# Moving one product of a two-tile feature pair, and starting its inner form one pair later

## The chip, the core and the metric

The kernel runs on one core of a Trainium2 chip. The metric is the device time of one execution in microseconds (us), the median of several runs. The engines are called TensorE (PE in the profile; PEld is its weight load), VectorE (DVE), ScalarE (ACT), GpSimd (POOL) and SyncE (SP, which here only issues DMAs).

## The reference, cut to what matters

One step of a hybrid decoder layer: a feed-forward network (FFN), a mixer (HGRN2 and Mamba-2 heads), a second FFN, a final norm. There are 1048 token rows (16 meta, 1024 prompt and 8 sample rows); the second FFN works on 1032 of them, since the meta rows are dropped. The change lies in the two FFNs alone:

```python
def swiglu(x, wg, wu, wd):
    return (jax.nn.silu(x @ wg) * (x @ wu)) @ wd
...
    h = h + 0.5 * swiglu(rmsnorm(h, n1), w1g, w1u, w1d)
...
    h = h + 0.5 * swiglu(rmsnorm(h, n2), w2g, w2u, w2d)
```

The model width is 1024 (8 blocks of 128), the FFN's width 2816 (22 feature tiles of 128). Everything is float32.

## The kernel before

**Arithmetic.** Each float32 factor is split into a high part (`hi`, a cast on ScalarE) and the remainder (`lo`, a subtraction on VectorE), and each product is made by three matmuls, hi x hi, hi x lo and lo x hi (`mm3`, L163 to L165).

**The seven products.** For one feature tile gate and up are computed together as a 2 x 2 by 2 x 2 block product in Winograd's form: seven products instead of eight, numbered 1 to 7, each over 4 blocks of 128 rows. The token columns are cut in two halves c = 0, 1, and each half in two quarters of Q columns (Q = 262 in the first FFN, 258 in the second). One *step* is one product for one half: 4 blocks x 3 matmuls = 12 matmuls of Q columns. The order of a tile is `ORDER = (1, 6, 2, 5, 7, 3, 4)`, two steps each. Products 1 and 2 are added up in one PSUM tile, 5 and 3 in one, 7 and 4 in one; 6 has its own. Such a tile ("acc") is a pair of banks, one for each half, and the pool has two of these pairs.

After the second half of a product, `post` in `pair` reads the PSUM pair: product 1 is copied by ScalarE (L675); 6 makes `v` (VectorE, L677); 2 is scaled to `g0` (L670) and goes through SiLU on ScalarE (L682); 5 makes `x` (L684); 7 makes `u1` (L686, then a scaling, L670); 3 makes `g1`; 4 makes `u0` (L699 in the inner form, L704 otherwise, then L670), and then the products gate x up are written (`product_`, L719).

**Pairs and the inner form.** The 22 tiles are taken as 11 pairs, numbered from 0. Pairs 0 and 1 are plain: two tiles with seven products each, 2 x 14 steps. From pair 2 on (the fifth tile) a pair is in the *inner form*: product 3 is left out of both tiles (`ORDER6`), and the two tiles' products 3 are made together, again in Winograd's form, as seven inner products of 6 matmuls each, in the "mis" banks (`Inner`, two at a step, the last one alone). An inner pair has thus 24 steps of 12 matmuls and 42 inner matmuls, 330 instead of 336. The first tile is products 1, 6, 2, 5, 7, 4; the second 1, 6, 2, 5, 7, then inner (1, 6) and (5, 7), then 4, then inner (2, 3) and (4). The SiLU of the third part and the last product of both tiles ("gates", `inner.then`) run in the first steps of the next pair.

`Inner.operands` builds once in each FFN, on VectorE (11 operations) and ScalarE (3 casts), the sums of the split token blocks that the inner products need, in the steps of pair 1, and one more operand (a cast and a remainder) in pair 2.

**The order of the work.** Inside an FFN the order on every engine is written out by hand. `Steps` is a list of TensorE's steps; `S.before(i, fn)` puts work ahead of step i, and what a step's `post` issues comes behind it. The engines run their queues in order and wait for one another by semaphores, so the list fixes only the order on each queue. `Left.plan` places a tile's weights: four loads (SyncE, L452) 11 and 10 steps ahead of the tile, the Winograd sums 5, 6, 7, 3 (VectorE, L458) 7 to 5 steps ahead, each cast (L462) 4 steps and each remainder (L466) 3 steps ahead of its product. `Hidden.jobs` makes the differences of the pair's results for the down projection (L816) and stores them to DRAM (SyncE, L819). Weights lie in 8 raw buffers ("r") and 6 split ones ("ws").

The program in these functions:

Of the kernel before, what the change touches and what calls it, by code (L numbers as in the profile page):

```python
# [313 lines left out]
ORDER = (1, 6, 2, 5, 7, 3, 4)  # L314
# [126 lines left out]
class Left:  # L441
# [27 lines left out]
        self.hi(p)  # L469
        self.lo(p)  # L470

    def plan(self, S, s0, late, sums, order=ORDER, last=0):
        n = len(order)
        his = [2 * i - 4 + late + last * (i == n - 1) for i in range(n)]
        for ps, ds, fn in (
            ((1, 7, 4, 2), (-11, -11, -10, -10), self.load),
            ((5, 6, 7, 3), [d + sums for d in (-7, -7, -6, -5)], self.sum_),
            (order, his, self.hi),
            (order, [d + 1 for d in his], self.lo),
        ):  # L480
            for p, d in zip(ps, ds):
                S.before(s0 + d, lambda p=p, fn=fn: fn(p))
# [9 lines left out]
class Unit:  # L492
# [25 lines left out]
    def both(self, S):  # L518
        for p in ORDER:
            for c in range(2):  # L520
                self.step(S, p, c, (0, 1))
# [6 lines left out]
ORDER6 = (1, 6, 2, 5, 7, 4)  # L528
# [121 lines left out]
def pair(K, S, wg, wu, f, ops, spread, hid, late_r, first=None, inner=None):  # L650

    nc = K.nc
    fs = slice(f * P, f * P + P)
    s0 = len(S.steps)
    wait = late_r > 14
    tm = {}  # L660
    left = Left(K, [wg[:, 0:4, fs], wu[:, 0:4, fs], wu[:, 4:8, fs], wg[:, 4:8, fs]], 4)

    def temp(n, cs):
        if n not in tm:
            tm[n] = halves(K.t(2 * K.Q))
        return tm[n][:, cs]

    def times_r(n, i, cs, src=None):
        t = temp(n, cs)
        nc.vector.tensor_mul(t, t if src is None else src, spread.lanes(i, cs))  # L670
        return t

    def post(p, cs, b):
        if p == 1:
            nc.scalar.copy(temp("z", cs), b)  # L675
        elif p == 6:
            nc.vector.tensor_add(temp("v", cs), b, temp("z", cs))  # L677
        elif p == 2 and (f == 0 or wait and f == 1):
            nc.scalar.copy(temp("g0", cs), b)
        elif p == 2:  # L680
            t = times_r("g0", 0, cs, b)
            nc.scalar.activation(t, t, AF.Silu)  # L682
        elif p == 5:
            nc.vector.tensor_add(temp("x", cs), b, temp("v", cs))  # L684
        elif p == 7:
            nc.vector.tensor_add(temp("u1", cs), b, temp("x", cs))  # L686
            if inner:
                times_r("u1", 1, cs)
        elif p == 3:
            nc.vector.tensor_add(temp("g1", cs), b, temp("v", cs))  # L690
            if f == 0:
                return
            if wait and f == 1:
                silu(0, cs)
            silu(1, cs)
            times_r("u1", 1, cs)
        elif inner:
            t = temp("v", cs)
            nc.vector.tensor_add(t, b, t)  # L699
            tm["u0"] = tm["v"]  # L700
            times_r("u0", 0, cs)
            product_(0, cs)
        else:
            nc.vector.tensor_add(temp("u0", cs), b, temp("v", cs))  # L704
            if f == 0:
                return
            times_r("u0", 0, cs)
            for n in range(2):
                product_(n, cs)

    def silu(n, cs):
        t = times_r(f"g{n}", n, cs)
        nc.scalar.activation(t, t, AF.Silu)  # L713

    def product_(n, cs):
        if "h" not in tm:
            tm["h"] = True
            hid.append(K.slot("s", K.T))
        nc.vector.tensor_mul(halves(hid[0][:, n * 2 * K.Q : n * 2 * K.Q + 2 * K.Q])[:, cs], temp(f"g{n}", cs), temp(f"u{n}", cs))  # L719

    if inner:
        i = f % 2
        left.plan(S, s0, 0, 0, ORDER6, 2 * i)
        unit = Unit(K, left.w, [o.op for o in ops], 4, post)

        def both(*ps):
            for p in ps:
                for c in range(2):
                    unit.step(S, p, c, (0, 1))

        def keep():
            inner.raw[i] = left.raw[3]

        cs = slice(0, 2)

        def gate():
            tm["g1"] = tm["x"]
            silu(1, cs)

        S.before(s0 - 4, keep)  # L740
        inner.then[i] = (gate, lambda: product_(1, cs))
        inner.out[i] = lambda: temp("x", cs)
        if i == 0:
            both(*ORDER6)
            return
        S.before(s0 + 1, lambda: inner.begin(S, s0))
        both(1, 6, 2, 5, 7)
        inner.step(S, 1, 6)
        inner.step(S, 5, 7)
        both(4)  # L750
        inner.step(S, 2, 3)
        inner.step(S, 4)
        e = len(S.steps)
        for at, fn in enumerate((inner.then[0][0], inner.then[1][0], inner.then[0][1], inner.then[1][1])):
            S.before(e + at, fn)
        return

    if not first:
        left.plan(S, s0, int(f == 1), 3 * int(f == 1))
        Unit(K, left.w, [o.op for o in ops], 4, post).both(S)  # L760
        return

    late = {}

    def post_first(p, cs, b):

        if p == 5:
            late[p] = b
        else:
            post(p, cs, b)  # L770
            if p == 6:
                post(5, cs, late[5])

    order = first(S, left)
    unit = Unit(K, left.w, [o.op for o in ops], 4, post_first)
    for ps_ in (order[:6], order[6:]):
        for c in range(2):
            for p in ps_:
                unit.step(S, p, c, (c,), True)
    cs = slice(0, 2)  # L780
    for i, (fn, *args) in enumerate(((silu, 0, cs), (silu, 1, cs), (times_r, "u0", 0, cs), (product_, 0, cs), (times_r, "u1", 1, cs), (product_, 1, cs))):
        S.before(s0 + late_r + i, lambda fn=fn, args=args: fn(*args))


FP = DFF // P // 2
# [5 lines left out]
class Hidden:  # L791
# [6 lines left out]
    def jobs(self, S, i, hid, e0, e1, inner):  # L798

        K = self.K  # L800
        t, b = {}, {}

        def block(n):

            return hid[n // 2][0][:, n % 2 * 2 * self.K.Q : n % 2 * 2 * self.K.Q + 2 * self.K.Q]

        def val(p):
            return b[p] if p in b else block({1: 0, 12: 1, 2: 2, 3: 3}[p])

        def sub(p, x, y):  # L810
            s = {5: 0, 6: 0, 7: 1, 4: 1}[p]
            if s not in t:
                t[s] = K.slot("s", self.K.T)
            o = (p in (6, 4)) * 2 * self.K.Q
            b[p] = t[s][:, o : o + 2 * self.K.Q]
            K.nc.vector.tensor_sub(b[p], val(x), val(y))  # L816

        def store(p):
            K.nc.sync.dma_start(self.d[p][:, :, i, :], halves(val(p)))  # L819

        ats = (e0 + 1, e1 + 1, e1 + 3, e1 + 5) if not inner else (e1 + 4, e1 + 5, e1 + 7, e1 + 9) if i < FP - 1 else (e1 + 4, e1 + 5, e1 + 6, e1 + 7)
        for at, args in zip(ats, ((5, 12, 1), (6, 3, 5), (7, 3, 12), (4, 2, 6))):
            S.before(at, lambda args=args: sub(*args))
            S.before(at + 2, lambda p=args[0]: store(p))
        for at, p in ((e0 + 2, 1), (e1 + (5 if inner else 1), 3), (e1 + 2, 2)):
            S.before(at, lambda p=p: store(p))

    def load(self, S, p, at):
# [147 lines left out]
def ffn(K, wg, wu, wd, ops, spread, src, first, after, late_r):  # L976
# [9 lines left out]
    with K.tc.manual_schedule(engines={E.PE, E.DVE, E.Activation, E.SP}):  # L986
        S = Steps()
        S.before(14, lambda: K.banks(2))
        hidden = Hidden(K)
        inner = Inner(K, ops)  # L990
        for i in range(NF // 2):
            hid, e = [], []
            rec = inner.next() if i >= 2 else None
            if i == 1:
                def operands(s0=len(S.steps)):
                    made, late = inner.operands()
                    for n, fn in enumerate(made):
                        S.before(s0 + 5 + 2 * n + n // 4, fn)
                    for n, fn in enumerate(late):
                        S.before(s0 + 36 + 2 * n, fn)  # L1000

                S.before(len(S.steps) + 4, operands)
            for f in (2 * i, 2 * i + 1):
                hid.append([])
                pair(K, S, wgv, wuv, f, ops, spread, hid[-1], late_r, first if f == 0 else None, rec)
                e.append(len(S.steps))
            hidden.jobs(S, i, hid, *([late_r + 6, max(late_r + 7, e[1])] if i == 0 else e), rec)
        h = []
        down(K, S, wdv, hidden, src, h, after)
        S.run()  # L1010
# [1253 lines left out]
```

## Time and profile before

| | |
|---|---|
| median of 3 runs | 2013.61 us (2012.29 to 2014.58) |
| the profiled execution | 2017.68 us, span 2016.0 us |
| granted TensorE clock, mean | 0.986 |
| TensorE busy | 1939.5 us (96%) |
| VectorE busy | 1543.0 us (77%) |
| ScalarE busy | 860.3 us (43%) |
| first FFN: pairs 1 and 2 | 78.45 to 124.05 us and 124.05 to 169.63 us |
| second FFN: pairs 1 and 2 | 1354.07 to 1394.37 us and 1394.37 to 1439.17 us |

Times in the profile count from the start of the span. A row of the timeline or of a group names engine, line, operation, tiles and shapes; a bracket at its end is the time that the engine stood idle just before, and what ended it. In a row by window stand the window, its length, the busy time and number of instructions of each engine, TensorE's granted clock, the share of the DMA engines and GB/s. In the list of waits stand who waited for whom, the sum in us, how often, and the longest. Matmuls overlap, and their ends are modelled, so the idle time shown is somewhat shorter than the time from one matmul's start to the next would say.

### The profile page before, as it was taken

The numbers are of one execution on the slowest core, as the hardware profiler recorded it, in microseconds if no ns is written. First come the engines' busy times: TensorE is split into PE (matmuls) and PEld (weight loads), VectorE is DVE, ScalarE is ACT, GpSimd is POOL, SyncE is SP. The second block draws the span as 40 slices with busy tenths as digits, with TensorE's granted clock in tenths as the row PEclk, the third lists the DMA queues.
The fourth block names the chain that finished last, engine by engine and source line by source line (L and its number), as shares of the span: only waits on it lengthen the run. The fifth ranks groups of instructions, "written<-read, shape, count | busy, mean of one in ns | idle before, by whom it ended". The sixth has DMA issues, their size and how long they took to land.

```text
span 2016.0 us, 40978 instructions
## 1 busy us (share of the span) xinstructions
PE 1939.5 (96%) x16573; PEld 1898.7 (94%) x16573; DVE 1543.0 (77%) x2744; ACT 860.3 (43%) x1653; POOL 85.0 (4%) x135
## 2 busy tenths in 40 slices
PE   7999999999999999999999999999999999999997
PEld 7989999999999999998988989999999999999997
DVE  7778888888788877576655447888888888878973
ACT  7523232223543644465543535743232322354352
POOL 4000000000000410000000001200000000000000
PEclk8999999999999999999998999999999999999999
DMA  7223233335877542232622154223232333487851
GB/s 215 77 88 102 85 105 100 95 96 157 252 248 245 158 151 55 58 100 71 169 77 75 56 165 135 73 91 112 79 106 85 105 101 103 143 236 245 272 180 65
DMA packets 323877, 258.45 MB, mean 128 GB/s; under 512 B 17568, under 2 KB 299424, under 8 KB 323680
## 3 DMA queue, kind: packets, MB, share of 16 engines
q1 hardware_dynamic: 323448, 255.79, 41.6%
q8 instruction: 131, 2.15, 0.5%
q14 instruction: 58, 0.48, 0.1%
q0 software_dynamic: 224, 0.04, 0.0%
q10 hardware_dynamic: 16, 0.00, 0.0%
HBM read 190.79 MB, written 65.05 MB: 127 GB/s over the span
## 4 chain that ended last, share of the span: by engine, by line
PE 52%; DVE 33%; issue 5%; DMA 5%; ACT 4%; SPq 0%; POOL 0%; DVEq 0%; ACTq 0%; POOLq 0%
PE acc L163 15%; PE acc L165 15%; PE acc L164 15%; DVE r L458 5%; DVE ws L466 4%; DVE t L670 2%; DVE u L844 2%; DVE s L719 2%; DMA r<-in_w_ffn_down_dram 2%; DVE ws L906 1%; DVE u L896 1%; DVE s L930 1%; DVE t L647 1%; DVE s L816 1%; DVE t L686 1%
## 5 line engine op out<-in xcount | busy, mean ns | idle before, releaser
L163 PE MATMUL acc<-u,ws 128*128 128x258 f32 (+4 forms) x4216 | 1239.6, 294 | 38.1 <-DVE t L686 24.3
L164 PE MATMUL acc<-u,ws 128*128 128x258 f32 (+4 forms) x4216 | 1227.8, 291 | 3.8 <-DVE u L352 2.0
L165 PE MATMUL acc<-u,ws 128*128 128x258 f32 (+4 forms) x4216 | 1227.2, 291 | 2.7 <-DVE ws L466 2.6
L163 PEld LDWEIGHTS acc<-u,ws 128*128 128x128 f32 x4216 | 802.8, 190 | 48.8 <-issue 38.9
L164 PEld LDWEIGHTS acc<-u,ws 128*128 128x128 f32 x4216 | 804.9, 191 | 6.4 <-DVE u L352 2.7
L165 PEld LDWEIGHTS acc<-u,ws 128*128 128x128 f32 x4216 | 802.1, 190 | 4.3 <-DVE ws L466 3.9
L466 DVE TENSOR_TENSOR ws<-r,ws 128x512 fp32r<-128x512 f32 x272 | 188.1, 692 | 32.9 <-ACT ws L462 32.8
L462 ACT CAST ws<-r 128x512 fp32r<-128x512 f32 x272 | 157.3, 617 | 15.1 <-ACT ws L462 9.9
L458 DVE TENSOR_TENSOR r<-r,r 128x512 f32<-128x512 f32 x176 | 121.2, 691 | 9.9 <-DMA r<-in_w_ffn_up_dram 7.9
L682 ACT ACTIVATE t<-t 128x516 f32<-128x516 f32 (+1 forms) x41 | 26.2, 640 | 203.7 <-DVE t L670 203.7
L844 DVE TENSOR_TENSOR u<-u,u 128x1048 fp32r<-128x1048 f32 (+3 forms) x84 | 97.1, 1158 | 9.2 <-ACT u L840 8.7
L713 ACT ACTIVATE t<-t 128x524 f32<-128x524 f32 (+1 forms) x47 | 29.8, 637 | 169.5 <-DVE t L670 169.5
L675 ACT COPY t<-acc 128x524 f32<-128x524 f32 (+3 forms) x46 | 26.1, 567 | 164.8 <-PE acc L165 164.8
L670 DVE TENSOR_TENSOR t<-t,u 128x524 f32<-128x524 f32 (+1 forms) x135 | 91.8, 697 | 2.8
L230 POOL TENSOR_TENSOR t<-t,t 128x262 f32<-128x262 f32 (+1 forms) x56 | 54.9, 990 | 845.0 <-ACT t L229 841.8
L158 DVE TENSOR_TENSOR ws<-r,ws 128x512 fp32r<-128x512 f32 x88 | 60.1, 693 | 35.3 <-ACT ws L157 34.8
L901 ACT CAST ws<-u 128x512 fp32r<-128x512 f32 (+1 forms) x72 | 42.2, 586 | 100.8 <-DVE u L896 93.2
L840 ACT CAST u<-u 128x1048 fp32r<-128x1048 f32 (+3 forms) x84 | 82.8, 988 | 3.6 <-DMA u<-hd 3.6
L930 DVE SCALAR_TENSOR_TENSOR s<-acc,s 128x524 f32<-128x524 f32 (+3 forms) x88 | 54.7, 644 | 36.3 <-PE acc L165 36.0
L901 ACT CAST ws<-r 128x512 fp32r<-128x512 f32 (+1 forms) x84 | 47.8, 581 | 64.8 <-DVE r L896 33.8
L906 DVE TENSOR_TENSOR ws<-r,ws 128x512 fp32r<-128x512 f32 (+1 forms) x84 | 57.4, 693 | 22.9 <-ACT ws L901 22.8
L157 ACT CAST ws<-r 128x512 fp32r<-128x512 f32 x88 | 53.7, 617 | 33.2 <-PE acc L165 29.0
(417 smaller groups left out, 2387.1 us busy)
## 6 DMA issues: line engine op xcount, KB each, us to landing
r<-in_w_ffn_down_dram SPq DMA_DIRECT2D x128, 256.0 KB
hd<-s SPq DMA_DIRECT2D x93, 258.0 KB
r<-in_w_ffn_gate_dram SPq DMA_DIRECT2D x88, 256.0 KB
r<-in_w_ffn_up_dram SPq DMA_DIRECT2D x88, 256.0 KB
hd<-s SPq DMA_DIRECT2D x77, 262.0 KB
u<-hd SPq DMA_DIRECT2D x36, 516.0 KB
u<-hd SPq DMA_DIRECT2D x28, 524.0 KB
r<-in_w_in_dram SPq DMA_DIRECT2D x56, 256.0 KB
```

Source lines behind the costliest of these rows:

```text
L163: mm(ps, whi, xhi, start=first, stop=False, skip_group_check=more)
L164: mm(ps, whi, xlo, start=False, stop=False, skip_group_check=more)
L165: mm(ps, wlo, xhi, start=False, stop=last, skip_group_check=more)
L458: self.K.nc.vector.tensor_tensor(self.raw[p], self.raw[x], self.raw[y], op)
L462: self.K.nc.scalar.copy(self.w[p][:, : self.n * P], self.raw[p])
L466: self.K.nc.vector.tensor_sub(t[:, 512 : 512 + w], self.raw[p], t[:, :w].bitcast(F32))
L670: nc.vector.tensor_mul(t, t if src is None else src, spread.lanes(i, cs))
L840: K.nc.scalar.copy(hi, lo.bitcast(F32))
L844: K.nc.vector.tensor_sub(lo, lo.bitcast(F32), hi.bitcast(F32))
L901: nc.scalar.copy(w[p, j, g][:, : n * P], src)
L906: nc.vector.tensor_sub(t[:, 512 : 512 + n * P], box[0], t[:, : n * P].bitcast(F32))
L930: nc.vector.scalar_tensor_tensor(t, b, 0.5, t, ALU.mult, ALU.add)
```

## The change

Four things, in both FFNs:

- In an inner pair, product 4 of the first tile is issued behind product 1 of the second: 1, 6, 2, 5, 7 | 1, (4 of the first), 6, 2, 5, 7, inner (1, 6), (5, 7), 4, inner (2, 3), (4). The first tile has 10 steps and the second 18. `Left.plan` takes the steps at which the products stand as a list instead of an extra distance for the last one; the second tile's loads and sums are moved by 1 to 2 steps against its own start, so that against the first tile's start the loads come one step earlier, the sum of product 3 one step later, and product 1's cast and product 4's change places.
- The inner operands are made every third step from the eighth step of pair 1 on, instead of about every second from the fifth; the last one 28 steps later, in pair 3.
- The inner form begins with pair 3 (the seventh tile) instead of pair 2.
- The gates and last products of a pair stand ahead of steps 0, 2, 3 and 5 of the next pair instead of 0, 1, 2 and 3; the differences and stores of `Hidden.jobs` move back by one or two steps.

```diff
-    def plan(self, S, s0, late, sums, order=ORDER, last=0):
-        n = len(order)
-        his = [2 * i - 4 + late + last * (i == n - 1) for i in range(n)]
+    def plan(self, S, s0, late, sums, order=ORDER, at=range(0, 14, 2)):
+        his = [i - 4 + late for i in at]
         for ps, ds, fn in (
-            ((1, 7, 4, 2), (-11, -11, -10, -10), self.load),
-            ((5, 6, 7, 3), [d + sums for d in (-7, -7, -6, -5)], self.sum_),
+            ((1, 7, 4, 2), (-10, -10, -9, -9) if sums == 2 else (-11, -11, -10, -10), self.load),
+            ((5, 6, 7, 3), [d + sums for d in (-7, -7, -6, -4 if sums == 2 else -5)], self.sum_),
...
-        left.plan(S, s0, 0, 0, ORDER6, 2 * i)
+        left.plan(S, s0, 0, 2 * i, ORDER6, ((0, 2, 4, 6, 8, 12), (0, 4, 6, 8, 10, 14))[i])
...
-        S.before(s0 - 4, keep)
+        S.before(s0, keep)
...
         if i == 0:
-            both(*ORDER6)
+            both(1, 6, 2, 5, 7)
+            inner.last = lambda: both(4)
             return
-        S.before(s0 + 1, lambda: inner.begin(S, s0))
-        both(1, 6, 2, 5, 7)
+        S.before(s0 + 3, lambda: inner.begin(S, s0 + 2))
+        both(1)
+        inner.last()
+        both(6, 2, 5, 7)
...
-        for at, fn in enumerate((inner.then[0][0], inner.then[1][0], inner.then[0][1], inner.then[1][1])):
+        for at, fn in ((0, inner.then[0][0]), (2, inner.then[1][0]), (3, inner.then[0][1]), (5, inner.then[1][1])):
             S.before(e + at, fn)
...
-        ats = (e0 + 1, e1 + 1, e1 + 3, e1 + 5) if not inner else (e1 + 4, e1 + 5, e1 + 7, e1 + 9) if i < FP - 1 else (e1 + 4, e1 + 5, e1 + 6, e1 + 7)
+        ats = (e0 + 1, e1 + 1, e1 + 3, e1 + 5) if not inner else (e1 + 4, e1 + 6, e1 + 8, e1 + 10) if i < FP - 1 else (e1 + 4, e1 + 6, e1 + 7, e1 + 8)
...
-        for at, p in ((e0 + 2, 1), (e1 + (5 if inner else 1), 3), (e1 + 2, 2)):
+        for at, p in ((e0 + (6 if inner else 2), 1), (e1 + (7 if inner else 1), 3), (e1 + 2, 2)):
...
-            rec = inner.next() if i >= 2 else None
+            rec = inner.next() if i >= 3 else None
             if i == 1:
-                def operands(s0=len(S.steps)):
+
+                def operands(s0=len(S.steps) + 8):
                     made, late = inner.operands()
                     for n, fn in enumerate(made):
-                        S.before(s0 + 5 + 2 * n + n // 4, fn)
+                        S.before(s0 + 3 * n, fn)
                     for n, fn in enumerate(late):
-                        S.before(s0 + 36 + 2 * n, fn)
-
-                S.before(len(S.steps) + 4, operands)
+                        S.before(s0 + 56 + 3 * n, fn)
+
+                S.before(len(S.steps) + 7, operands)
```

## The prediction

> **What bounds the kernel now.** I read the engine totals first, then TensorE's waits, then the waits of two stretches alone.
>
> ```profile
> PE 1939.5 (96%) x16573; PEld 1898.7 (94%) x16573; DVE 1543.0 (77%) x2744; ACT 860.3 (43%) x1653; POOL 85.0 (4%) x135
> ```
>
> TensorE is the bound: only 76 us of the 2016.0 us span are not its own. The list of TensorE's waits has one entry far ahead of all others; in the two stretches of steady inner pairs (169 to 520 us, first feed-forward network, FFN; 1439 to 1770 us, second) it is nearly alone:
>
> ```profile
> PE acc L163 <- DVE t L686: 24.3, 18, 1.5
> ```
> ```profile
> PE acc L163 <- DVE t L686: 10.3, 8, 1.3
> ```
> ```profile
> PE acc L163 <- DVE t L686: 12.2, 8, 1.5
> ```
>
> 18 waits are one for each inner pair (9 in each FFN). L686 is VectorE's read of product 7. In the first tile of an inner pair product 3 is missing, so 4 comes right behind 7 and adds into the same PSUM pair: it waits for that read, 10.3/8 = 1.29 us in the first FFN, 12.2/8 = 1.52 in the second. Next, the time of whole pairs (busy times by window; the first three rows are pairs 1, 2 and 3 of the first FFN, the last two pairs 1 and 2 of the second):
>
> ```profile
> 78.45:124.05 45.60, 42.30 (x339) 41.34 (x338) 39.63 (x63) 13.24 (x24) 0.00 (x0) 1.00 0.28 89
> 124.05:169.63 45.58, 42.19 (x332) 41.83 (x331) 36.09 (x61) 12.82 (x25) 0.00 (x0) 0.96 0.31 90
> 169.63:211.35 41.72, 40.43 (x332) 40.25 (x331) 35.17 (x61) 12.21 (x23) 0.00 (x0) 1.00 0.32 97
> ...
> 1354.07:1394.37 40.30, 40.30 (x338) 40.30 (x337) 35.41 (x56) 12.06 (x23) 0.00 (x0) 1.00 0.35 99
> 1394.37:1439.17 44.80, 41.53 (x333) 41.17 (x331) 35.70 (x60) 12.21 (x24) 0.00 (x0) 0.96 0.31 91
> ```
>
> An inner pair has 330 matmuls, a plain one 336, and yet the plain pair 1 of the second FFN (40.30 us, TensorE busy all the time, although the inner operands' VectorE work lies in it) beats every inner one. 40.30/28 gives a step (one product of one half, 12 matmuls) of 1.439 us there and, with 262 columns for 258, 1.461 in the first FFN. Pair 2, the first inner one, costs over 4 us more than a plain pair.
>
> **The moved product.** "acc" has two buffers, A and B, and a buffer freed first is given out first. First tile: 1 A, 6 B, 2 A, 5 B, 7 A. The new order then is 1' on B (a stroke marks the second tile), 4 on A, 6'. Product 4 comes 24 matmuls behind 7, so its wait is covered. But 6' opens a new group while 1' holds B until 2'; it must take A and wait until L699 has read product 4. The wait moves; it does not go. Its size depends on how late VectorE is.
>
> ```profile
> 309.39 0.28 PE L165 MATMUL acc<-u,ws 128*128 128x262 f32 x1
> 310.96 0.36 PE L163 MATMUL acc<-u,ws 128*128 128x262 f32 x1 [1.29 <-DVE t L686]
> ```
> ```profile
> 143.97 0.36 PE L163 MATMUL acc<-u,ws 128*128 128x262 f32 x1 [0.89 <-DVE t L686]
> ```
> ```profile
> 143.12 0.70 DVE L686 TENSOR_TENSOR t<-acc,t 128x524 f32<-128x524 f32 x1 [1.00 <-PE acc L165]
> ```
>
> At 143 us VectorE was idle and waited for TensorE: the wait is then 0.89 us, the least this dependence can cost. At 310 us VectorE was busy, hence 1.29. So I replay VectorE's queue in the new order from the steady pair that starts at 294.90 us.
>
> ```profile
> 296.79 1.31 DVE L670 TENSOR_TENSOR t<-t,u 128x524 f32<-128x524 f32 x2
> 298.70 0.69 DVE L466 TENSOR_TENSOR ws<-r,ws 128x512 fp32r<-128x512 f32 x1 [0.60 <-ACT ws L462]
> 299.31 1.31 DVE L719 TENSOR_TENSOR s<-t,t 128x524 f32<-128x524 f32 x2
> 300.54 0.69 DVE L466 TENSOR_TENSOR ws<-r,ws 128x512 fp32r<-128x512 f32 x1
> 301.14 0.70 DVE L677 TENSOR_TENSOR t<-acc,t 128x524 f32<-128x524 f32 x1
> 301.76 0.70 DVE L816 TENSOR_TENSOR s<-s 128x524 f32<-128x524 f32 x1
> 302.49 0.70 DVE L816 TENSOR_TENSOR s<-s,s 128x524 f32<-128x524 f32 x1
> 303.11 0.68 DVE L466 TENSOR_TENSOR ws<-r,ws 128x512 fp32r<-128x512 f32 x1
> 303.71 1.41 DVE L458 TENSOR_TENSOR r<-r,r 128x512 f32<-128x512 f32 x2
> 305.04 0.70 DVE L670 TENSOR_TENSOR t<-acc,u 128x524 f32<-128x524 f32 x1
> ...
> 309.52 0.68 DVE L466 TENSOR_TENSOR ws<-r,ws 128x512 fp32r<-128x512 f32 x1
> 310.12 0.70 DVE L686 TENSOR_TENSOR t<-acc,t 128x524 f32<-128x524 f32 x1
> ...
> 314.16 0.70 DVE L699 TENSOR_TENSOR t<-acc,t 128x524 f32<-128x524 f32 x1 [2.00 <-PE acc L165]
> ```
> ```profile
> 298.06 0.61 ACT L462 CAST ws<-r 128x512 fp32r<-128x512 f32 x1
> 298.57 0.64 ACT L713 ACTIVATE t<-t 128x524 f32<-128x524 f32 x1
> ```
>
> A VectorE operation starts 0.61 behind an independent one before it, 0.72 behind one it needs. The two gates (296.79) move from steps 0 and 1 to 0 and 2, their products (299.31) from 2 and 3 to 3 and 5. So the second gate now stands behind the cast's remainder at 298.70 and starts at 299.31; its SiLU (0.64) pushes ScalarE's next cast (0.61) to about 301.2, and the remainder of product 5's weights, at 300.54 above, to 301.24. L677 (product 6) slips 0.7 us to 301.85. Behind it stand a difference, the second product, a remainder and the two weight sums: L670 (the read of product 2, which frees A for 7) ends at about 306.3 instead of 305.74. TensorE wants A at 294.90 + 8 x 1.461 = 306.59, with 0.14 from VectorE's end to TensorE's start (310.82 to 310.96): room of 0.15. In the second FFN eight steps are 8 x 0.022 = 0.18 us shorter and VectorE's operations equally long, so I charge 0.1 us there.
> Then come difference, weight sum, a remainder that waits for its cast (ready about 307.5), and L684 near 308.2 to 308.9; 1' needs B at 309.51, which is new, room 0.5. L686 ends near 311.3, 4 needs A at 312.43. Behind it only four operations are left before L699, 2.6 us and a wait for one cast, for the 4.0 until product 4 ends at 315.35 (14 steps). So VectorE should be idle when L699 comes due, as it was at 314.16, and the wait is 0.89: gain 8 x (1.29 - 0.89) = 3.2 us in the first FFN and 8 x (1.52 - 0.89 - 0.1) = 4.2 in the second, **7.4** together. Bounds: nothing, if VectorE is as late as before; 22.5 if the wait went altogether.
> What else is moved with it: product 4's three operations (L699, L670, L719) come two steps later, close to the inner sums, and use up idle time such as the 2.00 us at 314.16; SyncE's store of block 1 waits for that L719 (end of step 14) and stands ahead of the next pair's loads, which VectorE sums in step 21, six steps or 8.7 us on; the second tile's loads go one step earlier, bound by free buffers as now. I cost these at nothing under that cover; without it a late load costs what the next part shows. Stores move by one or two steps and nobody waits for them but the last pair's, read back by the down projection (0.3 us each FFN).
>
> The wait I leave standing follows from one bank pair having one user. The Trainium skill, PSUM — Partial Sum Buffer, "PSUM bank collisions raise a hardware error", says to guard PSUM by bank, whatever the address. That speaks against a free move, and the rows agree: 4 adds to columns that L686 only reads, and still waits.
>
> **Pair 2 as a plain pair.** The seventh tile is pair 3's first, so pair 2 returns to 336 matmuls: 40.30 in the second FFN instead of 44.80 (4.5 us), and 40.30 x 262/258 = 40.93 instead of 45.58 in the first (4.65). Part of that gain must survive in pair 3, which is now the first inner one. What made pair 2 dear:
>
> ```profile
> 128.12 0.52 SPq L819 DMA_DIRECT2D hd<-s  x1
> ...
> 130.85 0.60 SPq L452 DMA_DIRECT2D r<-in_w_ffn_up_dram  x1
> ```
> ```profile
> 136.24 1.42 DVE L458 TENSOR_TENSOR r<-r,r 128x512 f32<-128x512 f32 x2 [2.53 <-DMA r<-in_w_ffn_up_dram]
> ```
> ```profile
> 138.42 0.36 PE L163 MATMUL acc<-u,ws 128*128 128x262 f32 x1 [2.50 <-DVE t L670]
> ```
> ```profile
> 126.00:134.00 8.00, 8.00 (x68) 8.00 (x67) 7.61 (x12) 1.64 (x3) 0.00 (x0) 1.00 0.52 148
> 138.50:141.70 3.20, 3.20 (x17) 3.20 (x18) 3.16 (x6) 3.04 (x6) 0.00 (x0) 0.58 0.01 4
> ```
>
> SyncE blocks on a store (128.12) that waits for VectorE, the second tile's loads queue behind it, VectorE stands 2.53 us for the load issued at 130.85, TensorE 2.50, and then the granted clock is 0.58 for 3.2 us: 17 matmuls where 26 fit (12 in 1.461), another 1.1 us at least. With the loads at steps 0 and 1 instead of 1 and 2, two go ahead of that store and the one in question right behind it, about 2 us sooner; the operands' VectorE work is over by then. I expect 0.3 us left of the 2.5 in each FFN, no clock drop, and 0.3 each for what the operands' five operations cost in pair 2: **9.15** less 1.2.
>
> The Trainium skill, TensorE: Matmul & The Clock Gate, "Why this matters for your kernels", puts the idle time that halves the clock at over about 3 us. By that, 2.50 us would have cost no clock and the gain would be 2 x 1.1 us smaller, 1999.6. The rows show the drop right behind 2.50 us, so the trace decides.
>
> **The operands further apart.** Pair 1 of the first FFN holds operand work at every second step from 5 on; now every third from 8 on, into pair 2.
>
> ```profile
> PE acc L163 <- DVE t L684: 2.2, 2, 1.5
> ```
> ```profile
> 115.84 1.42 DVE L458 TENSOR_TENSOR r<-r,r 128x512 f32<-128x512 f32 x2 [2.46 <-DMA r<-in_w_ffn_up_dram]
> ```
>
> The two waits in that pair (2.2 us) are late VectorE. The first should mostly go, with two operations fewer ahead of it; the second hangs on a DMA, and I count half of it. Bounds 0 and 2.2; I take **1.5**. The second FFN's pair 1 has nothing to gain.
>
> Sum: 7.4 + 9.15 + 1.5 - 1.2 - 0.6 (down projection) = 16.25 us. The profiled execution took 2017.68 us (the span of 2016.0 and 1.7 around it) and would take 2001.4; it stands 4.1 above the median of the runs shown, 2013.61, which becomes 1997.4.
>
> **The rivals.** *The inner pairs gain nothing*: VectorE is late at L699 as it was at L686, or 7 waits for L670. For it: room of 0.15 us; against it: four operations in 4.0 us. Without the 7.4 it is 2004.8.
> *The load's wait moves to pair 3, clock drop and all*: for it, pair 3 also follows a plain pair and the same store; against it, the earlier loads. Then 2 x (2.5 + 1.1 - 0.3) = 6.6 us come back: 2004.0.
> *Slower*: A is not free when 7 wants it, in all 16 inner pairs. If L670 slips by three more VectorE operations (1.95 us at 0.65), less the room, 16 x 1.8 = 29 us are lost, on top of the wait that stays: 2026. It outweighs the forecast from 1.02 us in each pair, and is slower beyond 0.2% from 1.3 us. For it: VectorE runs without a gap from 298.70 to 312; against it: the same operations in nearly the same number.
> *The wait goes altogether*, that is, 6' does get a free buffer: 16 x 0.89 more plus the 0.1s, 1982.4. Two buffers speak against it.
>
> **How the numbers follow.** Forecast 0.55 (its own range 1992 to 2002), no gain in the inner pairs 0.18, the load's wait in pair 3 0.12, slower 0.11, all gone 0.04. 0.2%, about what can be told from no change, is 4 us. Faster: 0.55, 0.04, and most of the second and third, 0.22: 0.81. Same: the rest of these, 0.08. Slower 0.11. A range of 1992 to 2009 leaves out the slower case, the all-gone case and small ends.
>
> **What would show it.** Right: 16 waits of about 0.9 us of L163 for L699 and none for L686; pairs 3 to 10 near 41.3 and 40.8 us; pair 2 near 41; no clock under 1 near 138 and 1409 us. Wrong: waits for L670 or L684 in each inner pair, L699 waits over 1.3 us, or VectorE idle on a weight load in pair 3.

## The result, and the profile after

| | |
|---|---|
| median after, 4 runs | 1998.43 us (1996.57 to 2002.89) |
| median before, 4 runs beside them | 2014.09 us (2012.29 to 2017.92) |
| after / before | 0.9923, 95% interval 0.99 to 0.9946 |
| the profiled execution | 1997.03 us, span 1995.2 us, granted clock 0.992 |

The forecast was 1997.4 us, with 0.81 on faster: the time came out 1.0 us above it. Whether it did so for the reasons given has to be read from the parts. All lines of the program below the edits have new numbers: product 7's read, L686 before, is L685 after; product 4's, L699, is L698; L670 is L669, L684 is L683, L677 is L676.

The engine totals, then TensorE's waits over the whole span and over the steady inner pairs of the first FFN (165 to 497 us) and of the second (1424 to 1751 us):

```profile
PE 1931.3 (97%) x16585; PEld 1889.7 (95%) x16585; DVE 1532.8 (77%) x2720; ACT 858.9 (43%) x1647; POOL 83.1 (4%) x135
```
```profile
PE acc L163 <- DVE t L698: 14.1, 16, 0.9
...
PE acc L163 <- DVE t L683: 3.0, 2, 2.0
```
```profile
PE acc L163 <- DVE t L698: 7.1, 8, 0.9
PE mis L163 <- DVE t L643: 0.6, 1, 0.6
```
```profile
PE acc L163 <- DVE t L698: 7.0, 8, 0.9
PE mis L163 <- DVE t L643: 0.7, 1, 0.7
```

The 18 waits for product 7's read (24.3 us) are gone (one of 0.28 us is left, in the plain pair 1 of the first FFN), and an entry for product 4's read has come in their place: 16 waits, one for each of the 8 inner pairs of each FFN, with a mean of 0.88 us and a longest one of 0.9. No wait for L669 (product 2's read) stands in either stretch.

Whole pairs by window, in the form of the rows shown for before: pairs 1, 2, 3 and 4 of the first FFN, then pairs 1 to 4 of the second.

```profile
78.94:123.84 44.90, 42.05 (x338) 41.23 (x337) 38.44 (x62) 13.37 (x25) 0.00 (x0) 1.00 0.29 90
123.84:165.39 41.55, 41.17 (x338) 40.98 (x337) 34.09 (x54) 12.21 (x23) 0.00 (x0) 1.00 0.38 110
165.39:206.76 41.37, 40.48 (x333) 40.30 (x332) 34.19 (x57) 11.59 (x22) 0.00 (x0) 1.00 0.30 87
206.76:248.10 41.34, 40.45 (x332) 40.27 (x331) 35.10 (x61) 12.31 (x23) 0.00 (x0) 1.00 0.32 96
...
1342.81:1383.09 40.28, 40.28 (x338) 40.28 (x337) 34.38 (x55) 11.66 (x22) 0.00 (x0) 1.00 0.34 99
1383.09:1423.99 40.90, 40.55 (x338) 40.37 (x337) 33.71 (x54) 12.11 (x23) 0.00 (x0) 1.00 0.38 111
1423.99:1464.64 40.65, 39.77 (x332) 39.60 (x331) 33.85 (x57) 11.57 (x22) 0.00 (x0) 1.00 0.30 87
1464.64:1505.41 40.77, 39.89 (x332) 39.65 (x331) 34.87 (x61) 12.26 (x23) 0.00 (x0) 1.00 0.32 98
```

The granted clock is 1.00 in every one of them; it was 0.96 in both pairs 2 before. Summed from the starts of the pairs, pair 1 to the down projection went from 426.00 to 418.15 us in the first FFN and from 416.40 to 408.21 in the second:

| us, both FFNs together | before | after | gain | counted in the prediction |
|---|---|---|---|---|
| pair 1 | 85.90 | 85.18 | 0.7 | 1.5 |
| pair 2 | 90.39 | 82.45 | 7.9 | 7.95 |
| pairs 3 to 10 | 666.1 | 658.7 | 7.4 | 7.4 |
| sum | 842.4 | 826.4 | 16.0 | 16.85, less 0.6 for the down projection |

The spans of the two profiled executions differ by 20.8 us; the 4.8 beyond these 16.0 lie outside the changed code (3.9 of them between the two FFNs). The medians differ by 15.7, and the interval of the ratio means 11 to 20 us. So the change is worth about 16 us, and the parts in the table add up to that.

### The profile page after: what moved, and what is told of

It is laid out like the page before. It is cut to its first block, busy times and chain, and to the rows that moved or that the text cites. A ratio compares the mean times of both kernels' runs of the same rounds, so it can differ in the third digit from the quotient of the medians.

```text
span 1995.2 us, 40967 instructions
## 1 busy us (share of the span) xinstructions
PE 1931.3 (97%) x16585; PEld 1889.7 (95%) x16585; DVE 1532.8 (77%) x2720; ACT 858.9 (43%) x1647; POOL 83.1 (4%) x135
## 3 DMA queue, kind: packets, MB, share of 16 engines
q8 instruction: 131, 2.15, 0.5%
## 4 chain that ended last, share of the span: by engine, by line
PE 79%; DVE 12%; DMA 4%; ACT 2%; issue 2%; SPq 0%; POOL 0%; DVEq 0%; ACTq 0%; POOLq 0%
PE acc L163 23%; PE acc L165 23%; PE acc L164 23%; PE mis L163 1%; PE mis L165 1%; PE mis L164 1%; DMA r<-in_w_ffn_down_dram 1%; DVE u L352 1%; DVE s L932 1%; DVE ws L466 1%; DVE u L846 1%; DMA r<-in_w_ffn_up_dram 1%; DMA s<-in_x_prompt_dram 1%; DVE ws L908 1%; DVE t L698 1%
## 5 line engine op out<-in xcount | busy, mean ns | idle before, releaser
L163 PE MATMUL acc<-u,ws 128*128 128x258 f32 (+3 forms) x4248 | 1246.7, 294 | 23.3 <-DVE t L698 14.1
L164 PE MATMUL acc<-u,ws 128*128 128x258 f32 (+3 forms) x4248 | 1234.6, 291 | 3.1 <-DVE u L352 2.5
L165 PE MATMUL acc<-u,ws 128*128 128x258 f32 (+3 forms) x4248 | 1233.6, 291 | 3.5 <-DVE ws L466 3.4
L669 DVE TENSOR_TENSOR t<-t,u 128x524 f32<-128x524 f32 (+1 forms) x135 | 92.9, 697 | 2.8
L908 DVE TENSOR_TENSOR ws<-u,ws 128x512 fp32r<-128x512 f32 (+1 forms) x72 | 47.4, 659 | 26.5 <-ACT ws L903 26.5
```

What stands on the lines that cost most here:

```text
L163: mm(ps, whi, xhi, start=first, stop=False, skip_group_check=more)
L164: mm(ps, whi, xlo, start=False, stop=False, skip_group_check=more)
L165: mm(ps, wlo, xhi, start=False, stop=last, skip_group_check=more)
L908: nc.vector.tensor_sub(t[:, 512 : 512 + n * P], box[0], t[:, : n * P].bitcast(F32))
```

## Experiments

Four questions were open: which part of the change pair 2's gain needs, whether the wait for product 4's read is a buffer's wait and nothing else, how thin the cover of product 2's read is, and why pair 1 gave less than counted. Each ratio is against the kernel before, measured beside it, with its 95% interval.

### 1. The moved product without the later start of the inner form

After, with the inner form from pair 2 on, and the inner operands where they were:

```diff
-            rec = inner.next() if i >= 3 else None
+            rec = inner.next() if i >= 2 else None
...
-                def operands(s0=len(S.steps) + 8):
+                def operands(s0=len(S.steps)):
...
-                        S.before(s0 + 3 * n, fn)
+                        S.before(s0 + 5 + 2 * n + n // 4, fn)
...
-                        S.before(s0 + 56 + 3 * n, fn)
+                        S.before(s0 + 36 + 2 * n, fn)
...
-                S.before(len(S.steps) + 7, operands)
+                S.before(len(S.steps) + 4, operands)
```

> The changed kernel with the inner form from pair 2 on and the operands at their old steps: only product 4, its weights, gates and stores are moved. Theory (the wait moves to 6' and shrinks to 0.9 us, and the second tile's earlier loads alone take the wait for a weight load and the clock drop out of the first inner pair): 18 waits for product 4's read of 0.9 us, pairs 3 to 10 near 41.3 and 40.8 us, pair 2 near 42 us in both networks instead of 45.6 and 44.8; in all 7 us from the inner pairs and 6 to 7 from pair 2, about 2000.5. Rival (pair 2's cost came from the operands' VectorE work and from following a plain pair, whatever the loads do): the same 7 us, pair 2 still over 44 us with a low clock behind a wait of 2 us or more, about 2007.

Measured: 1999.38 us (1997.48 to 2001.84), ratio 0.9931 (0.9914 to 0.9947): not told apart from after. Pair 2 by window, first and second FFN:

```profile
121.75:163.09 41.34, 40.45 (x333) 40.27 (x332) 35.80 (x60) 12.58 (x24) 0.00 (x0) 1.00 0.29 87
...
1383.12:1423.74 40.62, 39.74 (x332) 39.57 (x331) 35.51 (x60) 12.13 (x23) 0.00 (x0) 1.00 0.30 88
```

Pair 2 is an inner pair here, and takes 41.34 and 40.62 us, no more than the plain one of after (41.55 and 40.90). TensorE's only wait in it is the new one, 0.9 us for product 4's read; no load is waited for, and the clock is 1.00. So pair 2 need not be plain to have its gain: here it is its own second tile whose loads go a step earlier. (In after, pair 2 is plain, and its loads stand at the steps where a plain pair's stood before.) With the inner form a pair later and the operands further apart, the time is the same.

### 2. The later start and the spread operands without the moved product

Before, with the other two parts of the change alone (the diff of experiment 1 the other way round):

```diff
-            rec = inner.next() if i >= 2 else None
+            rec = inner.next() if i >= 3 else None
...
+                def operands(s0=len(S.steps) + 8):
...
+                        S.before(s0 + 3 * n, fn)
...
+                        S.before(s0 + 56 + 3 * n, fn)
...
+                S.before(len(S.steps) + 7, operands)
```

> The kernel before with the inner form from pair 3 on and the operands at their new steps; product order, loads, gates and stores as before. Theory: the waits for product 7's read stay at 1.3 and 1.5 us; pair 2 falls to about 41 us, but pair 3, now the first inner one, with its loads behind the stores again, stands 1.5 to 2.5 us and drops its clock: 44 to 45 us. Net 0 to 4 us faster, 2010 to 2014. Rival (the operands' work made the load's wait): pair 3 shows no wait over 1.6 us, and the kernel is 8 to 9 us faster, about 2005.

Measured: 2009.11 us (2006.01 to 2014.05), ratio 0.9977 (0.9963 to 0.9991), 4.7 us less than the median before: between the two expectations. Pair 2, plain and with no load moved, has its gain here too, and TensorE waits for nothing in it:

```profile
123.39:164.70 41.31, 41.18 (x338) 41.00 (x337) 34.06 (x55) 12.25 (x23) 0.00 (x0) 1.00 0.33 98
...
1386.62:1427.05 40.43, 40.43 (x338) 40.38 (x337) 33.72 (x54) 12.11 (x23) 0.00 (x0) 1.00 0.33 99
```

But the load's wait moved into pair 3. TensorE's waits from 164 to 499 us, and the two rows behind the second of them on VectorE and TensorE:

```profile
PE acc L163 <- DVE t L686: 10.0, 8, 1.3
PE acc L163 <- DVE t L670: 1.1, 1, 1.1
```
```profile
175.51 1.42 DVE L458 TENSOR_TENSOR r<-r,r 128x512 f32<-128x512 f32 x2 [2.85 <-DMA r<-in_w_ffn_up_dram]
...
177.69 0.36 PE L163 MATMUL acc<-u,ws 128*128 128x262 f32 x1 [1.13 <-DVE t L670]
```

VectorE stands 2.85 us for the same load as before (2.53 there), but TensorE only 1.13 us (1.32 in the second FFN) instead of 2.50, and the clock is not cut. The load goes out 5.8 us into the pair here (at 170.47 us; the pair starts at 164.70), a microsecond sooner than in pair 2 of before (6.8). That this is because VectorE has no operand work ahead of the stores is likely, but no run tried it alone. Pair 3 takes 43.17 and 42.68 us, 1.4 over the steady pairs. The rival of the prediction, the wait going on to pair 3, happens when the later start stands alone, but without the drop of the clock.

### 3. After, with the second tile's loads a step later

```diff
-            ((1, 7, 4, 2), (-10, -10, -9, -9) if sums == 2 else (-11, -11, -10, -10), self.load),
+            ((1, 7, 4, 2), (-9, -9, -8, -8) if sums == 2 else (-11, -11, -10, -10), self.load),
```

> The changed kernel with the four weight loads of an inner pair's second tile one step later, where they stood before (steps 1, 1, 2, 2 of the first tile). Theory: steady inner pairs do not care (their loads wait for free buffers anyway), pair 3 alone gets a wait for the load of 1 to 2.5 us in each network, with a low clock behind it if it reaches 2 us: 2 to 7 us slower than the changed kernel, 2000 to 2005. Rival (the loads' step is of no account): within 1 us of the changed kernel, 1998.

Measured: 2000.11 us (1998.15 to 2003.88), ratio 0.9936 (0.9918 to 0.9953). The medians of this and of after can't be told apart, but pair 3 shows what the step is worth: 42.94 and 42.40 us for 41.37 and 40.65. Its rows on VectorE and TensorE, and the window just behind them:

```profile
176.68 1.42 DVE L458 TENSOR_TENSOR r<-r,r 128x512 f32<-128x512 f32 x2 [3.06 <-DMA r<-in_w_ffn_up_dram]
...
178.86 0.36 PE L163 MATMUL acc<-u,ws 128*128 128x262 f32 x1 [1.33 <-DVE t L669]
```
```profile
179.00:182.40 3.40, 3.40 (x29) 3.40 (x30) 2.78 (x6) 2.47 (x5) 0.00 (x0) 1.00 0.02 6
```

The load's wait is back (1.33 and 1.48 us), and behind it the granted clock stays at 1.00. It did not reach the 2 us for which the expectation named a low clock.

### 4. Before, with the second tile's loads alone a step earlier

```diff
-    def plan(self, S, s0, late, sums, order=ORDER, last=0):
+    def plan(self, S, s0, late, sums, order=ORDER, last=0, early=0):
...
-            ((1, 7, 4, 2), (-11, -11, -10, -10), self.load),
+            ((1, 7, 4, 2), [d - early for d in (-11, -11, -10, -10)], self.load),
...
-        left.plan(S, s0, 0, 0, ORDER6, 2 * i)
+        left.plan(S, s0, 0, 0, ORDER6, 2 * i, i)
```

> The kernel before with nothing changed but the four weight loads of an inner pair's second tile, one step earlier (steps 0, 0, 1, 1 of the first tile). Theory (these loads, queued behind a store, are the whole reason why the first inner pair took 45.6 and 44.8 us): pair 2 shows no wait for a load and no low clock, 41.7 to 42.5 us in the first network and 41.3 to 42 in the second; the 18 waits for product 7's read stay at 1.3 and 1.5 us; 6 to 7 us faster than before, about 2007.5. Rival (it took the moved product or the later stores as well): pair 2 still over 43 us, under 3 us gained.

Measured: 2006.14 us (2004.34 to 2010.31), ratio 0.9967 (0.9953 to 0.9982), 6.2 us less than before. SyncE's queue at the start of pair 2, and the pair by window in both FFNs:

```profile
126.96 0.53 SPq L819 DMA_DIRECT2D hd<-s  x1
127.58 0.56 SPq L452 DMA_DIRECT2D r<-in_w_ffn_up_dram  x1
128.30 0.43 SPq L452 DMA_DIRECT2D r<-in_w_ffn_gate_dram  x1
```
```profile
122.90:164.80 41.90, 40.59 (x332) 40.41 (x331) 35.89 (x61) 12.81 (x25) 0.00 (x0) 1.00 0.29 86
...
1385.01:1425.70 40.69, 39.78 (x332) 39.60 (x331) 35.52 (x60) 12.13 (x23) 0.00 (x0) 1.00 0.29 87
```

The load that VectorE waited for was issued at 130.85 us before, 6.8 us into the pair and behind two stores; here it goes at 127.58, 4.7 us into the pair. Its sum no longer waits, and pair 2 falls from 45.58 to 41.90 and from 44.80 to 40.69 us, as an inner pair in the old order. So this one step of the loads, with nothing else, gives pair 2 as much as the whole change does: 7.8 us by the profile, against 7.9. The steady pairs stay at 41.77 and 41.3, so what they gained in after is the moved product's.

### 5. One more VectorE operation in each inner pair

After, with an operation of 128 x 524 added ahead of step 5 whose result nobody reads:

```diff
         if i == 0:
+            def more():
+                x = spread.tile()[:, : 2 * K.Q]
+                nc.vector.tensor_mul(K.t(2 * K.Q), x, x)
+            S.before(s0 + 5, more)
```

> The changed kernel with one more VectorE operation (a product of two 128 x 2Q tiles, 0.70 us, read by nobody) in each of the 16 inner pairs, ahead of the weight sums in step 5. Theory (the room in front of product 7 is 0.2 us in the first network and nothing in the second, as the replay of VectorE's queue has it): product 2's read comes 0.61 us later and product 7 waits for it, 0.4 us in each pair of the first network and 0.6 in the second; the waits for product 4's read stay at 0.89: 8 us slower than the changed kernel, about 2006.5. Rival (VectorE's idle time in the pair takes it up): no new wait, under 2 us.

Measured: 2006.06 us (2002.34 to 2009.73), ratio 0.9963 (0.9951 to 0.9976). TensorE's waits in pairs 4 to 10 (203 to 499 us, then 1466 to 1763 us):

```profile
PE acc L163 <- DVE t L698: 6.2, 7, 0.9
PE acc L163 <- DVE t L669: 1.9, 7, 0.3
```
```profile
PE acc L163 <- DVE t L698: 6.2, 7, 0.9
PE acc L163 <- DVE t L669: 3.5, 7, 0.5
```

A new wait for product 2's read (L669) appears in 7 of the 8 inner pairs of each FFN, 0.27 us in the first and 0.50 in the second, and the old one stays. The pairs grow by more than the idle time shown; pair 4 of each FFN, 41.34 and 40.77 us in after:

```profile
205.82:247.67 41.85, 40.70 (x332) 40.34 (x331) 35.74 (x62) 12.31 (x23) 0.00 (x0) 1.00 0.31 96
1470.64:1512.01 41.37, 39.99 (x332) 39.64 (x331) 35.49 (x62) 12.25 (x23) 0.00 (x0) 1.00 0.32 97
```

One operation takes up 0.61 us of VectorE's queue, and a pair is 0.5 us longer in the first FFN and 0.6 in the second: the room was about 0.1 us in the first FFN, and none in the second. Pair 3, which follows a plain pair and so has no gates of an inner one in its first steps, has no such wait. The mechanism of the prediction's slower rival is real and begins one operation away.

### 6. The gates where they stood before

```diff
-        for at, fn in ((0, inner.then[0][0]), (2, inner.then[1][0]), (3, inner.then[0][1]), (5, inner.then[1][1])):
+        for at, fn in ((0, inner.then[0][0]), (1, inner.then[1][0]), (2, inner.then[0][1]), (3, inner.then[1][1])):
```

> The changed kernel with the gates and last products of a pair ahead of steps 0, 1, 2 and 3 of the next one, as before. Theory (their respacing was a cost of 0.7 us to product 6's read that fell within the room, and no gain): product 6's read 0.7 us earlier, product 7's buffer free a little earlier or at the same time, no wait gone or added but the 0.1 us in the second network; within 1 us of the changed kernel, 1997.5 to 1998.5. Rival (the respacing is needed since the gates' waits for ScalarE sit in front of product 2's read): product 7 waits in each pair, 3 us or more slower.

Measured: 1997.9 us (1996.17 to 1999.34), ratio 0.9918 (0.9891 to 0.9945), the same as after. The 16 waits are unchanged. In the second FFN a steady pair is 0.1 us shorter than the 40.77 of after:

```profile
1467.66:1508.32 40.66, 39.78 (x332) 39.60 (x331) 34.90 (x61) 12.16 (x23) 0.00 (x0) 1.00 0.32 98
```

That is the 0.1 us charged in the prediction for the later second gate, too short to stand in the list of waits; it was there, and it buys nothing.

### 7. A buffer of its own for product 6 of the second tile

After, with that one product in two of the "mis" banks, one for each half, so that it needs no "acc" pair:

```diff
-                self.ps[b, cs] = (K.psm() if mis and b == 7 else K.psum())[:, None, :self.K.Q]
+                self.ps[b, cs] = (K.psm() if mis and (b == 7 or K.pairs) else K.psum())[:, None, :self.K.Q]
...
-        both(6, 2, 5, 7)
+        for c in range(2):
+            unit.step(S, 6, c, (c,), True)
+        both(2, 5, 7)
```

> The changed kernel with product 6 of an inner pair's second tile accumulated in two single mis banks instead of the acc pair that product 4 has just left (its read by VectorE becomes two operations of half the length). Theory (the wait of 0.9 us is for that buffer alone and VectorE has room): all 16 waits go, each 1.05 us from matmul start to matmul start beyond the usual spacing: about 16 us faster than the changed kernel, near 1982. Rival (VectorE is the second bound just behind): the wait comes back elsewhere in the pair, behind the reads of products 2, 5 or 7, and the gain is under 8 us, over 1990.

Measured: 1977.88 us (1976.45 to 1978.94), ratio 0.9823 (0.9808 to 0.9837). TensorE's only wait from 120 to 485 us, one steady pair of each FFN, and the two reads on VectorE:

```profile
PE mis L163 <- DVE t L643: 0.6, 1, 0.6
```
```profile
203.97:244.20 40.23, 40.23 (x332) 40.23 (x331) 35.10 (x62) 12.31 (x23) 0.00 (x0) 1.00 0.33 100
1452.41:1492.06 39.65, 39.65 (x332) 39.58 (x331) 34.85 (x62) 12.26 (x23) 0.00 (x0) 1.00 0.33 102
```
```profile
224.61 0.70 DVE L698 TENSOR_TENSOR t<-acc,t 128x524 f32<-128x524 f32 x1 [1.05 <-PE acc L165]
...
227.50 0.42 DVE L676 TENSOR_TENSOR t<-mis,t 128x262 f32<-128x262 f32 x1
```

All 16 waits are gone, and TensorE is busy for the whole of a pair. VectorE reads product 4 exactly as before (it waits 1.05 us for TensorE ahead of it), so nothing but the shared buffer made TensorE wait. This version beats before by 35.9 and after by about 20 us; 1.1 in each steady pair, 17.9 in pairs 3 to 10 of both FFNs by the profiles. Pairs 1 and 2, which the edit leaves alone, give another 1.5, which is within their scatter from run to run.

### 8. The same, with the loads of pair 2's first tile two steps earlier

```diff
-        left.plan(S, s0, int(f == 1), 3 * int(f == 1))
+        left.plan(S, s0, int(f == 1), 3 * int(f == 1), early=2 * int(f == 4))
```

(`early` is taken off the four loads' steps, as in experiment 4.)

> The kernel with product 6 in the mis banks (1977.9 us) and, in addition, the weight loads of pair 2's first tile two steps earlier, ahead of pair 1's stores of block 1 and of the first difference. Theory (VectorE's wait for a load at 115 us, and TensorE's 1.3 to 2.0 us behind it, come from SyncE holding the loads behind those stores): that wait goes in the first network, nothing changes in the second: 1.3 to 2 us less, about 1976. Rival (the load lands late for its own sake, by what else the DMA engines carry then): the wait stays, 1978.

Measured: 1978.28 us (1977.6 to 1978.91), ratio 0.9824 (0.9802 to 0.9846), the same as without it. In after, SyncE had two stores to issue from 105.05 us on, the second at 107.50, when its data was there; the load went out behind them, VectorE stood 3.02 us and TensorE 2.01:

```profile
105.05 2.96 SPq L821 DMA_DIRECT2D hd<-s  x2
108.10 0.56 SPq L452 DMA_DIRECT2D r<-in_w_ffn_gate_dram  x1
108.79 1.04 SPq L452 DMA_DIRECT2D r<-in_w_ffn_up_dram  x2
...
115.60 1.42 DVE L458 TENSOR_TENSOR r<-r,r 128x512 f32<-128x512 f32 x2 [3.02 <-DMA r<-in_w_ffn_up_dram]
...
117.77 0.36 PE L163 MATMUL acc<-u,ws 128*128 128x262 f32 x1 [2.01 <-DVE t L683]
```

With the loads ahead of the second store the wait is gone, and pair 1 falls from 44.15 us (experiment 7) to 42.57; but pair 2 grows from 40.98 to 41.70, and 0.9 us of the whole is below what a median of four runs resolves here. In the 0.7 that pair 2 gives back there is a wait of 0.51 us for ScalarE's cast of an operand (L564), which experiment 7's pair 2 doesn't have; why it arises was not followed up.

### 9. The buffer of its own, with the inner form from pair 2 on

Experiments 1 and 7 together.

> The kernel with product 6 in the mis banks, with the inner form from pair 2 on again and the operands at their old steps. Theory (once the wait inside is gone, an inner pair takes its 330 matmuls, 40.2 us in the first network, and beats a plain one, so the later start now costs): pair 2 at 40.2 and 39.6 to 39.8 us with no wait for a load, about 1.5 us less in all, 1976.5. Rival (an inner pair right behind the operands' work, with no idle time left in front of it, is held up by VectorE): pair 2 over 41 us, 1978 or more.

Measured: 1978.21 us (1973.94 to 1981.28), ratio 0.9826 (0.9808 to 0.9843), not told apart from experiment 7. Pair 2 takes 40.30 and 39.50 us, against 40.98 and 40.75 as a plain pair: without the wait the inner form is 0.7 to 1.25 us shorter; its 6 matmuls fewer, half a step, are 0.73 of that.

## Why the prediction was right, and where its reasons were not

**The inner pairs: right in every step.** The wait moved from product 7's read to product 4's and became what the dependence itself costs. None of the other parts does this: without the moved product (experiments 2 and 4) the steady pairs stay as they were. The steady pair of after that answers to the one replayed in the prediction starts at 206.76 us, and this is VectorE's queue in it:

```profile
213.64 0.69 DVE L676 TENSOR_TENSOR t<-acc,t 128x524 f32<-128x524 f32 x1
...
217.41 0.69 DVE L669 TENSOR_TENSOR t<-acc,u 128x524 f32<-128x524 f32 x1
...
222.36 0.70 DVE L685 TENSOR_TENSOR t<-acc,t 128x524 f32<-128x524 f32 x1
...
225.64 0.69 DVE L466 TENSOR_TENSOR ws<-r,ws 128x512 fp32r<-128x512 f32 x1 [0.64 <-ACT ws L462]
...
227.39 0.70 DVE L698 TENSOR_TENSOR t<-acc,t 128x524 f32<-128x524 f32 x1 [1.05 <-PE acc L165]
```
```profile
228.24 0.36 PE L163 MATMUL acc<-u,ws 128*128 128x262 f32 x1 [0.89 <-DVE t L698]
```

Counted from the pair's start, product 6's read starts at 6.88 us (replayed: 301.85 - 294.90 = 6.95), product 2's ends at 11.34 (replayed 11.4; TensorE wants the buffer at 11.69), product 7's ends at 16.30 (replayed 16.4). VectorE is idle ahead of L698, and the wait is 0.89. Pairs 3 to 10 gained 3.12 us in the first FFN (3.2 counted) and 4.26 in the second (4.2). Experiment 7 shows that the wait was for the buffer. It doesn't bear out the prediction's rule of one user for a bank whatever the address, and neither do the rows of before: 6' overwrites the very columns that product 4's read takes, as 4 added to those that product 7's read took, so a rule that goes by address gives the same wait. Experiment 5 shows that the room at product 2's read was about 0.1 us in the first FFN and none in the second, as thin as written. The slower rival was not far off: one more operation of VectorE begins it.

**Pair 2: right in what it does, its size in part by luck, and the later start not needed.** In after, pair 2 gains by being plain, with its loads where a plain pair's stood before, as the prediction says; experiment 2 has that gain without any load moved (41.31 and 40.43 us). That the earlier loads keep the wait from going on to pair 3 is right too (experiments 2 and 3). What the section "Pair 2 as a plain pair" has wrong is its ground for the later start, that a plain pair beats an inner one. The earlier loads alone, with pair 2 in the inner form, take the same stall away (experiments 1 and 4), and on top of them the later start gains nothing: experiment 1's time is not told apart from that of after. The comparison that misled was of a plain pair with an inner pair 2 that held a stall of 2.5 us and a cut clock; the row of pair 3 (41.72), an inner pair without them, stood beside it. With the wait of 0.9 us still there, the inner pair 2 of experiment 1 (41.34 and 40.62) lies among the plain ones of the other runs (40.98 to 41.91 and 40.43 to 40.90 in seven profiles); without that wait it is 0.7 to 1.25 us shorter than the plain one (experiment 9).

That 7.93 us came out where 7.95 were counted is luck in its parts. The plain pairs took 41.55 and 40.90 us, not 40.93 and 40.30, which is 1.2 more in all; and of the 1.2 charged, the 0.6 for a rest of the load's wait in pair 3 did not appear, while the 0.6 for operands lie near what is there, 0.38 and 0.35 us of TensorE waiting for ScalarE's cast of an operand (L564).

**The rival with the load's wait in pair 3** is half shown. Without the earlier loads the wait does go there (experiments 2 and 3), 1.1 to 1.5 us long instead of 2.5, with no drop of the clock. Its price is then about 1.4 to 1.75 us for each pair 3, about 3 in all by the profiles, not 6.6.

**Pair 1 of the first FFN: 0.7 instead of 1.5, and even that is not shown to come from the change.** The wait that should go, 0.77 us, went, and one of 0.28 us for another read (L685) came close behind it; the one counted by half grew from 1.46 to 2.01. Its load still stood behind a waiting store in SyncE's queue (the rows under experiment 8) and went out at 108.8 us, 108.9 before, so that TensorE, now earlier, only waited longer for it. Over the runs profiled here pair 1 takes 43.79 to 45.59 us with the operands in the old places (four profiles) and 43.89 to 44.90 with the new ones (six): the ranges cover each other. Experiment 1, without the spread, is not told apart from after. So the spread of the operands has no effect that could be measured.

**The down projection: no loss.** The waits in pair 10 are 0.61 and 0.67 us, 0.64 and 0.70 before, and in the 119 us behind the end of pair 10 TensorE waits for nothing in either FFN, before or after. The 0.6 us taken off were not there.

Together: 7.4 us from the moved product; 7.9 from pair 2 without its stall, of which the earlier loads keep about 3 from being lost again in pair 3; and the two small terms nearly cancel: 0.8 too much for pair 1, 0.6 too little for the down projection.

## What to carry to other kernels

When a change bundles several edits, ask of each stall which edit alone would take it away: here a stall of 2.5 us and its cut clock hung on one DMA issue behind a store that waits in the same queue. Either of two edits took it out of pair 2. The later start alone left about half of it to the next pair; four loads a step earlier left none, and nothing for the later start to gain. Moving work behind a wait on a buffer moves the wait to the next user of that buffer, down to the dependence itself; only another buffer takes it away, and that was worth 20 us more. Before a replay's small room is trusted, measure it by adding one operation to the engine whose queue it depends on.

## What was not expected of the hardware

The drop of the granted clock came behind the 2.50 and 2.39 us of idle time on TensorE in the two pairs 2 of before (0.58 and 0.54 over 3.2 us), and not behind 2.01 us in pair 1 of after, nor behind 1.1 to 1.5 us in experiments 2 and 3. This is the window right behind the 2.01 us:

```profile
118.00:121.40 3.40, 3.40 (x29) 3.33 (x29) 3.40 (x7) 0.00 (x0) 0.00 (x0) 1.00 0.00 0
```

29 matmuls run in it at full clock, against 17 in 3.20 us behind the 2.50. But the length of the idle time does not decide it alone. In the mixer of experiment 2's kernel TensorE stood 2.28 us until 947.51 us, and 2.15 us until 1086.35 us; these are the windows right behind:

```profile
947.50:951.00 3.50, 3.49 (x108) 3.25 (x108) 2.98 (x9) 1.78 (x5) 0.00 (x0) 1.00 0.57 161
...
1086.80:1090.10 3.30, 3.30 (x43) 3.26 (x35) 3.30 (x5) 0.00 (x0) 0.00 (x0) 0.50 0.66 158
```

The longer one left the clock at 1.00, the shorter one had it at 0.50. What else it depends on, these runs don't say; the prediction's rival had taken the drop as certain wherever the load is late.

The other surprise is how even the least cost of the dependence is: TensorE to VectorE's read of 128 x 524 (516 in the second FFN) and back to TensorE shows as 0.88 to 0.89 us of idle time in all 16 places, with VectorE waiting, and costs 1.1 us of a pair (41.34 to 40.23, and 40.77 to 39.65, by experiment 7).
